# Reading and writing a matmul's columns alternately from two halves, in runs of two

## The chip, the cores and the metric

One core of a Trainium2 chip runs the whole program. The metric is device time in microseconds (us), the median of several runs. The kernel before has 2062.7 us, from three runs of 2062.58, 2063.46 and 2062.70 us.

## The reference, cut to what matters

One inference step of a two-layer decoder trunk, for 512 prompt tokens and 8 x 4 sample tokens (544 tokens, model width 1024, hidden width 2816). Everything is float32.

```
h = h + 0.5 * swiglu(rmsnorm(h, ffn1_norm[i]), w1, w3, w2)      # four such FFNs, two a layer
xn = rmsnorm(h, mix_norm[i])
layer 0: mix = (u * (w_s @ rmsnorm(v) + b_s)) @ w_out,  u, v = split(xn @ w_in)    # gMLP
layer 1: mix = attention(rmsnorm(xn @ w_q), shared k, v, log-forget) @ w_o         # forgetting attention
h = h + mix
h = h + 0.5 * swiglu(rmsnorm(h, ffn2_norm[i]), w1, w3, w2)
h = h + sigmoid(rmsnorm(h, ple_norm[i]) @ w_gate) * (pe[i] @ w_proj)               # gated embedding (PLE)
after layer 0: k, v, logf = shared_kv(h)
...
swiglu(x, w1, w3, w2) = (silu(x @ w1) * (x @ w3)) @ w2
```

## The kernel before, in words

The activations lie transposed: 128 features on the partitions, 544 tokens along the free dimension. A float32 product is made of three products in the type fp32r (float32 operands, read by TensorE in reduced precision): both operands are split into a high and a low part, and high x high, high x low and low x high are summed in one PSUM accumulator. The text calls each of the three a *split product*: one MATMUL with 128 x 128 weights (loaded by its own LDWEIGHTS) and a moving operand of 128 partitions by N tokens. 15,724 of the 16,442 MATMULs in the trace are such fp32r products; the others are transposes, the small float32 products of the gMLP's spatial gate, of the statistics and of the sample tokens' attention.

Three groups of lines hold nearly all of them. `mm` (lines 241, 245 and 247) is the plain product over all 544 tokens: since a PSUM bank has room for 512 columns, the tokens are cut by `COLS` at `CUT` into 256 and 288 columns, and `whole` places the two pieces on both sides of the border between the two banks of a `ps` tile. `products` inside `ffn_steps` (line 491) holds the FFN's first two weights in a seven-product form (a Strassen-like scheme on token halves and on halves of the inner dimension): it works on halves of `HT` = 272 tokens already. The remaining split products are the statistics (`rstd`, line 362), the last tile (`cols_mm`, 675), the value projection (`v_group`, 829 to 831, 256 columns), the scores and outputs of the attention (`qk`, 1107 to 1115, and `pv`, 1159 to 1161, 256 to 512 columns) and the output projection (`product`, 1268 to 1275, 272 columns).

VectorE (DVE) and ScalarE (ACT) split weights and activations, evacuate PSUM and do the elementwise work beside TensorE; weights come by DMA from the SyncE (SP) queue. In the FFNs the order of work is written out by hand (a slot list, run under a manual schedule); elsewhere the framework's scheduler sets it. Operands are read, and results written, in ascending address order in all these products:

```
i = nc.tensor.matmul(out[:, a:b], wh, xh[:, a:b], start=s, stop=False)
```

Of the kernel before, what the change touches and what calls it, by code (L numbers as in the profile page):

```python
# [82 lines left out]

CUT = 256
COLS = ((0, CUT), (CUT, T))


def whole(p):  # L90
# [4 lines left out]
class Builder:  # L95
# [133 lines left out]
    def mm(self, out, w, x, first, last, mid=None):  # L229

        nc = self.nc
        out = whole(out)
        n = len(w)
        pin, self.pins = self.pins > 0 and first, self.pins - first
        for k in range(n):
            (wh, wl), (xh, xl) = w[k], x[k]
            if mid is not None and k == n - 1:
                mid()
            s, e = first and k == 0, last and k == n - 1
            for a, b in COLS:  # L240
                i = nc.tensor.matmul(out[:, a:b], wh, xh[:, a:b], start=s, stop=False)  # L241
                if pin and k == 0:
                    self.tc.keep_in_program_order(i)
            for a, b in COLS:
                nc.tensor.matmul(out[:, a:b], wh, xl[:, a:b], start=False, stop=False)  # L245
            for a, b in COLS:
                nc.tensor.matmul(out[:, a:b], wl, xh[:, a:b], start=False, stop=e)  # L247

    def tile_mm(self, xs, mid=None):

# [103 lines left out]
    def rstd(self, acc):  # L354

        parts = self.tmp(F32R), self.tmp(F32R)
        self.nc.scalar.copy(parts[0], acc)
        self.nc.vector.tensor_tensor(parts[1], acc, parts[0].bitcast(F32), ALU.subtract)
        sums = [self.pb()[:, :HT] for _ in range(2)]
        for n, x in enumerate(parts):  # L360
            for a, ps in enumerate(sums):
                self.nc.tensor.matmul(ps, self.onesr, x[:, a * HT:(a + 1) * HT], start=n == 0, stop=n == 1)
        r = self.st()
        assert self.chain is None
        self.chain = self.rsqrt_steps(r, sums, D)
        next(self.chain)
        return r
# [97 lines left out]
    def ffn_steps(self, h, xf, rstd, hid, todo, plain, on_chunk):  # L465
# [8 lines left out]
        def products(j, k, part):  # L474
            if k == "1" and j not in tiles:
                tiles[j] = {}
            t = tiles[j]
            if k in "152" and "ABC"["125".index(k)] not in t:
                if k == "2":
                    t["B"] = [self.pb()[:, :HT] for _ in range(2)]  # L480
                else:
                    t["A" if k == "1" else "C"] = self.ps()[:, :, :HT]
            out = t["A" if k in "1674" else "C" if k in "53" else "B"]
            dst = out if k == "2" else [out[:, w] for w in range(2)]
            hi, lo = self.take()
            for kp in range(NKP):
                xh, xl = xf[kp][k]
                for n, (a, b) in enumerate(((hi, xh), (hi, xl), (lo, xh))):
                    for w in range(2):
                        c = slice(512 * w + P * kp, 512 * w + P * kp + P)  # L490
                        nc.tensor.matmul(dst[w], a[:, c], b, start=k in "152" and kp == 0 and n == 0,  # L491
                                         stop=kp == NKP - 1 and n == 2, skip_group_check=True)
            after.append(lambda: evict(j, k))

# [175 lines left out]
    def cols_mm(self, outs, w, x):  # L670

        for (a, b), out in zip(COLS, outs):
            for k, ((wh, wl), (xh, xl)) in enumerate(zip(w, x)):
                for n, (u, v) in enumerate(((wh, xh), (wh, xl), (wl, xh))):
                    i = self.nc.tensor.matmul(out[:, :b - a], u, v[:, a:b], start=k == 0 and n == 0,
                                              stop=k == len(w) - 1 and n == 2)
                    if k == n == a == 0:
                        self.tc.keep_in_program_order(i)
# [89 lines left out]
    def kv(self, h, box, ffn_gain):  # L768
# [40 lines left out]
        def v_group(g, beside):  # L809
# [13 lines left out]
            for i in range(4):  # L823
                if i % 2 == 0:
                    self.advance()
                t, out = slice(i * P, i * P + P), p[:, 256 * i:256 * i + 256]
                for k, (wh, wl) in enumerate(w):
                    xh, xl = xs[k]
                    nc.tensor.matmul(out, xh[:, t], wh, start=k == 0, stop=False)  # L829
                    nc.tensor.matmul(out, xh[:, t], wl, start=False, stop=False)  # L830
                    nc.tensor.matmul(out, xl[:, t], wh, start=False, stop=k == NC_ - 1)  # L831
                for f in beside[i]:
                    f()
            for i in range(4):
# [245 lines left out]
    def attention(self, xs, acc, h_out, on_chunk):  # L1080
# [19 lines left out]
        def qk(h):  # L1100
            kp, _ = st["kv", h]
            qp = st.pop(("q", h))
            S = [self.ps(), self.ps()]
            for i in range(4):
                out = S[i // 2][:, i % 2, :]
                w, qs = W[i], slice(i * P, (i + 1) * P)
                nc.tensor.matmul(out[:, :w], self.L[h % 4][:, qs], self.R[:, 0, :w],
                                 start=True, stop=False)
                nc.tensor.matmul(out[:, :w], qp[:, 0, qs], kp[:, 0, :w], start=False, stop=False)
                nc.tensor.matmul(out[:, :w], qp[:, 0, qs], kp[:, 1, :w], start=False, stop=False)  # L1110
                nc.tensor.matmul(out[:, :w], qp[:, 1, qs], kp[:, 0, :w], start=False, stop=False)
                if i == 0:
                    nc.tensor.matmul(out[:, :256], self.identr, self.neg[:, 128:384], start=False, stop=True)
                else:
                    nc.tensor.matmul(out[:, (i - 1) * P:(i + 1) * P], self.identr, self.neg[:, 0:256],
                                     start=False, stop=True)
            if h < 4:
                self.fetch_term(h + 4)
            ps = []
            for i in range(4):  # L1120
                w = (i + 1) * P
                sc = S[i // 2][:, i % 2, :w]
                m, l = self.sm(1), self.sm(1)
                p = self.tmp()
                nc.vector.tensor_reduce(m, sc, AX.X, ALU.max, negate=True)
                nc.scalar.activation(p[:, :w], sc, AF.Exp, bias=m, accum_out=l)
                nc.vector.reciprocal(l, l)
                if i in (1, 2):
                    nc.gpsimd.tensor_scalar(p[:, :w], p[:, :w], l, None, ALU.mult)
                else:  # L1130
                    nc.scalar.activation(p[:, :w], p[:, :w], AF.Copy, scale=l)
                ps.append(p)
            st["p", h] = ps
# [17 lines left out]
        def pv(h):  # L1151
# [4 lines left out]
            for j, (t3, c0, n) in enumerate(mv):  # L1156
                vs = slice(j * P, (j + 1) * P)
                out = acc[:, 512 - n:512]
                nc.tensor.matmul(out, vp[:, 0, vs], t3[:, 0, c0:c0 + n], start=j == 0, stop=False)
                nc.tensor.matmul(out, vp[:, 0, vs], t3[:, 1, c0:c0 + n], start=False, stop=False)  # L1160
                nc.tensor.matmul(out, vp[:, 1, vs], t3[:, 0, c0:c0 + n], start=False, stop=j == 3)
            o[h] = self.big(F32R)
            self.split_pair(o[h], acc, slice(0, SEQ))

# [94 lines left out]
            for a in range(2):  # L1259
                nc.sync.dma_start(out=st["vs"][NS * a:NS * a + NS], in_=self.vsd[:, 512 * a:512 * a + 512])  # L1260

        def product(out, hs, w, ks, late=False):
            hi, lo = w
            pin, self.pins = self.pins > 0, 0
            for n, k in enumerate(ks):
                c = slice(P * n, P * n + P)
                s, e = n == 0, n == len(ks) - 1
                i = nc.tensor.matmul(out, hi[:, c], o[k][:, 0, hs], start=s, stop=False)  # L1268
                if pin and s:
                    self.tc.keep_in_program_order(i)  # L1270
                if not late:
                    nc.tensor.matmul(out, hi[:, c], o[k][:, 1, hs], start=False, stop=False)  # L1272
                nc.tensor.matmul(out, lo[:, c], o[k][:, 0, hs], start=False, stop=e and not late)  # L1273
            for n, k in enumerate(ks if late else ()):
                nc.tensor.matmul(out, hi[:, P * n:P * n + P], o[k][:, 1, hs], start=False, stop=n == len(ks) - 1)

        def project_half(c, part):

# [1 line left out]
            hi, lo = self.unit()  # L1280
            for a in range(2):
                w = slice(4 * P * a, 4 * P * a + 4 * P)
                product(p[:, a, :HT], slice(0, HT), (hi[:, w], lo[:, w]), range(4 * part, 4 * part + 4))
            out = self.hp[c][:, :, :HT]
            behind = st.pop(("sel", 1), None)
            with self.tc.issue_after(behind.ins) if behind else nullcontext():
# [4 lines left out]
        def project(c):  # L1291

            p = self.ps()
            self.pins = c == 0
            product(p[:, 0, :HT], slice(HT, T), self.unit(), range(NH), late=c == 0)
            out = h_out[c][:, HT:]
            nc.vector.tensor_tensor(out, p[:, 0, :HT], out, ALU.add)
            on_chunk(c, slice(HT, T))
# [230 lines left out]
```

## Time and profile before

| what | value |
|---|---|
| median of three runs | 2062.7 us |
| the profiled execution's span, first to last instruction | 2060.8 us |
| around the span, by the median | 1.9 us |
| TensorE (PE), busy share of the span | 99% |
| weight loads (PEld), busy share | 98% |
| VectorE (DVE), busy share | 73% |
| ScalarE (ACT), busy share | 46% |
| GpSimd (POOL), busy share | 9% |
| mean DMA rate | 115 GB/s |

The profiled execution's own device time is not given apart from its span, so its time is taken as the span and the 1.9 us around it.

How to read it: PE's busy time is no measure of its rate. MATMULs overlap, and the profile models their ends: a product has a "duration" of 288 ns while the next one starts 125 ns after it. What a product costs is the distance from its start to the next one's start, read from rows that give a time and a count (the chain in order of time, or the timeline of TensorE).

### The profile page before, as it was taken

The page shows a single profiled execution, that of the slowest core. Times are in us where ns is not written, and L with a number is a line of the kernel's source. Part 1 is how long each engine was busy: PE and PEld are TensorE (multiplying, and loading weights), DVE is VectorE, ACT ScalarE, POOL GpSimd, SP SyncE. Part 2 cuts the span into 40 slices and gives each one's busy share as a digit, 9 for nine tenths or more (in the row PEclk, how much of TensorE's full clock was granted, in tenths as well). Part 3 has the DMA queues.
Part 4 walks back from the last instruction along what each step waited for, and adds up shares of the span by engine and source line. Part 5 has one row for each costly group of instructions (what it writes and reads, how often), then busy time and mean ns, then how long its engine had stood idle before and what let it go on. Part 6 is the DMA issues. An engine that isn't in the chain of part 4 may idle for free.

```text
span 2060.8 us, 38864 instructions
## 1 busy us (share of the span) xinstructions
PE 2045.6 (99%) x16442; PEld 2013.9 (98%) x16442; DVE 1506.0 (73%) x1862; ACT 950.9 (46%) x1421; POOL 185.6 (9%) x222
## 2 busy tenths in 40 slices
PE   9999999999999999999999999999999999999999
PEld 8999999999999999999999999999987999999999
DVE  7877777556687778776688777776476888777774
ACT  7535344423554344454456343534364754344451
POOL 0000000410100000043060000001131200000020
PEclk9999999999999999999999999999999999999999
DMA  5233234312223232432374323324669232222421
GB/s 185 84 111 107 74 109 141 97 45 83 83 93 113 72 104 82 154 99 82 103 261 161 113 86 110 107 66 136 192 211 320 96 100 84 102 103 82 130 97 44
DMA packets 93823, 237.95 MB, mean 115 GB/s; under 512 B 9538, under 2 KB 27490, under 8 KB 93650
## 3 DMA queue, kind: packets, MB, share of 16 engines
q1 hardware_dynamic: 93506, 235.44, 34.3%
q8 instruction: 129, 2.11, 0.4%
q14 instruction: 44, 0.36, 0.0%
q10 hardware_dynamic: 144, 0.04, 0.0%
HBM read 218.95 MB, written 16.49 MB: 114 GB/s over the span
## 4 chain that ended last, share of the span: by engine, by line
PE 92%; DVE 3%; ACT 2%; issue 1%; DMA 1%; SPq 0%; POOL 0%; DVEq 0%; ACTq 0%; POOLq 0%
PE ps L491 33%; PE ps L241 16%; PE ps L247 16%; PE ps L245 15%; PE pb L491 5%; DVE big L199 1%; ACT big L198 1%; PE ps L1268 1%; PE ps L1273 1%; PE ps L1272 1%; DVE big L184 0%; PE ps L1223 0%; PE ps L829 0%; PE ps L830 0%; PE ps L831 0%
## 5 line engine op out<-in xcount | busy, mean ns | idle before, releaser
L491 PE MATMUL ps<-big,big 128*128 128x272 f32 x5616 | 727.6, 288 | 1.8 <-DVE big L508 1.3
L491 PEld LDWEIGHTS ps<-big,big 128*128 128x128 f32 x5616 | 714.2, 188 | 2.4 <-issue 1.6
L199 DVE TENSOR_TENSOR big<-big,big 128x1024 fp32r<-128x1024 f32 (+2 forms) x538 | 590.8, 1100 | 106.4 <-ACT big L198 106.0
L198 ACT CAST big<-big 128x1024 fp32r<-128x1024 f32 (+2 forms) x538 | 488.0, 932 | 267.8 <-DVE big L184 262.5
L241 PE MATMUL ps<-big,big 128*128 128x256 f32 (+1 forms) x2684 | 558.2, 289 | 1.2 <-ACT big L198 0.8
L247 PE MATMUL ps<-big,big 128*128 128x256 f32 x2684 | 554.0, 288 | 1.9 <-DVE big L199 1.9
L245 PE MATMUL ps<-big,big 128*128 128x256 f32 x2684 | 553.8, 287 | 0.1
L241 PEld LDWEIGHTS ps<-big,big 128*128 128x128 f32 x2684 | 429.8, 188 | 5.3 <-issue 1.7
L247 PEld LDWEIGHTS ps<-big,big 128*128 128x128 f32 x2684 | 429.3, 188 | 3.7 <-DVE big L199 3.2
L245 PEld LDWEIGHTS ps<-big,big 128*128 128x128 f32 x2684 | 432.3, 189 | 0.5 <-DVE big L298 0.5
L326 POOL TENSOR_TENSOR st<-st,tmp 128x544 f32<-128x544 f32 (+1 forms) x63 | 89.0, 1412 | 1587.0 <-ACT tmp L324 1586.8
L530 DVE SCALAR_TENSOR_TENSOR big<-ps,big 128x544 f32<-128x544 f32 x160 | 115.5, 722 | 106.6 <-PE ps L247 106.4
L184 DVE TENSOR_TENSOR big<-big,big 128x1024 f32<-128x1024 f32 x156 | 190.0, 1218 | 0.0
L499 ACT COPY tmp<-ps 128x544 f32<-128x544 f32 x117 | 71.9, 614 | 141.3 <-PE ps L491 141.3
L454 ACT ACTIVATE big<-big 128x544 f32<-128x544 f32 x88 | 58.0, 660 | 163.0 <-DVE big L451 161.8
L491 PE MATMUL pb<-big,big 128*128 128x272 f32 x936 | 124.0, 288 | 0.0
L451 DVE TENSOR_TENSOR big<-big,st 128x1088 f32<-128x1088 f32 x88 | 113.3, 1289 | 10.6 <-ACT big L513 8.9
L491 PEld LDWEIGHTS pb<-big,big 128*128 128x128 f32 x936 | 120.2, 188 | 0.0
L286 DVE TENSOR_TENSOR big<-big,big 128x544 fp32r<-128x544 f32 (+1 forms) x112 | 81.5, 734 | 36.7 <-ACT big L285 36.5
L297 ACT ACTIVATE big<-big,gains 128x544 fp32r<-128x544 f32 (+1 forms) x80 | 55.6, 704 | 105.9 <-DVE big L530 64.9
L298 DVE SCALAR_TENSOR_TENSOR big<-big,gains,big 128x544 fp32r<-128x544 f32 (+1 forms) x80 | 66.7, 843 | 25.2 <-ACT big L297 25.2
L285 ACT CAST big<-big 128x544 fp32r<-128x544 f32 (+1 forms) x112 | 71.3, 644 | 16.2 <-DVE big L457 8.9
(213 smaller groups left out, 1436.5 us busy)
## 6 DMA issues: line engine op xcount, KB each, us to landing
big<-in_w SPq DMA_DIRECT2D x156, 512.0 KB
big<-in_w2a SPq DMA_DIRECT2D x64, 512.0 KB
big<-in_w2b SPq DMA_DIRECT2D x32, 384.0 KB
big<-in_w13p SPq DMA_DIRECT2D x16, 512.0 KB
big<-in_win SPq DMA_DIRECT2D x16, 512.0 KB
big<-in_wg SPq DMA_DIRECT2D x16, 512.0 KB
big<-in_ck SPq DMA_DIRECT2D x16, 512.0 KB
big<-in_cv SPq DMA_DIRECT2D x16, 512.0 KB
```

The source lines that it names most:

```text
L184: self.nc.vector.tensor_tensor(t, a, b, ALU.add if op == "+" else ALU.subtract)
L198: self.nc.scalar.copy(hi, src)
L199: self.nc.vector.tensor_tensor(lo, src, hi.bitcast(F32), ALU.subtract)
L241: i = nc.tensor.matmul(out[:, a:b], wh, xh[:, a:b], start=s, stop=False)
L245: nc.tensor.matmul(out[:, a:b], wh, xl[:, a:b], start=False, stop=False)
L247: nc.tensor.matmul(out[:, a:b], wl, xh[:, a:b], start=False, stop=e)
L286: self.nc.vector.tensor_tensor(pair[:, 1, cols], src, pair[:, 0, cols].bitcast(F32), ALU.subtract)
L326: nc.gpsimd.tensor_tensor(acc[:, cols], acc[:, cols], sq, ALU.add)
L451: tt(g, g, rstd.unsqueeze(1).broadcast_to([P, 2, T]), ALU.mult)
L491: nc.tensor.matmul(dst[w], a[:, c], b, start=k in "152" and kp == 0 and n == 0, stop=kp == NKP - 1 and n == 2, skip_group_check=True)
L499: nc.scalar.copy(t["r" + k], t["C" if k == "5" else "A"])
L530: nc.vector.scalar_tensor_tensor(h[c], whole(out), 0.5, h[c], ALU.mult, ALU.add)
```

## The change

Two functions are added. `woven` views an access pattern of N columns as pairs from two halves: columns 0 and 1, then N/2 and N/2 + 1, then 2 and 3, then N/2 + 2 and N/2 + 3, and so on. `product` issues the MATMUL with this view on the moving operand and on the result, so that each sum still arrives in its own place. All 15,724 split products go through `product`; transposes and float32 products do not. With it `CUT` goes from 256 to `HT` = 272, so the token pieces in `mm` and in the last tile are 272 and 272 and not 256 and 288. An inner function named `product` is renamed `products`.

```diff
-CUT = 256
+CUT = HT
 COLS = ((0, CUT), (CUT, T))
+def woven(ap):
+    return ap.rearrange("p (a b c) -> p b a c", a=2, c=2)
+def product(nc, out, w, x, **k):
+    return nc.tensor.matmul(woven(out), w, woven(x), **k)
...
             for a, b in COLS:
-                i = nc.tensor.matmul(out[:, a:b], wh, xh[:, a:b], start=s, stop=False)
+                i = product(nc, out[:, a:b], wh, xh[:, a:b], start=s, stop=False)
...
-                        nc.tensor.matmul(dst[w], a[:, c], b, start=k in "152" and kp == 0 and n == 0,
+                        product(nc, dst[w], a[:, c], b, start=k in "152" and kp == 0 and n == 0,
                                          stop=kp == NKP - 1 and n == 2, skip_group_check=True)
...
-                    nc.tensor.matmul(out, xh[:, t], wh, start=k == 0, stop=False)
+                    product(nc, out, xh[:, t], wh, start=k == 0, stop=False)
...
-                nc.tensor.matmul(out[:, :w], qp[:, 0, qs], kp[:, 0, :w], start=False, stop=False)
+                product(nc, out[:, :w], qp[:, 0, qs], kp[:, 0, :w], start=False, stop=False)
```

The same replacement is made on all the other lines named above.

No instruction is added or taken away, and the order stays on every engine; what changes on TensorE is the pattern. Line numbers below line 86 move up by 10 or 11, and all split products carry line 97, that of `product`. In the first FFN tile of `mm` TensorE had these rows, one weight block (`ps_190` the accumulator, `big_120` the moving operand, `big_123` and `big_124` the high and low weights):

```order
L241 MATMUL ps_190<-big_120,big_123 128x256
L241 MATMUL ps_190<-big_120,big_123 128x288
L245 MATMUL ps_190<-big_120,big_123 128x256
L245 MATMUL ps_190<-big_120,big_123 128x288
L247 MATMUL ps_190<-big_120,big_124 128x256
L247 MATMUL ps_190<-big_120,big_124 128x288
```

Now it has the following ones for this and the next two blocks (68 steps, two halves, two columns):

```order
L97 MATMUL ps_190<-big_120,big_123 128x68x2x2 x4
L97 MATMUL ps_190<-big_120,big_124 128x68x2x2 x2
L97 MATMUL ps_190<-big_127,big_123 128x68x2x2 x4
L97 MATMUL ps_190<-big_127,big_124 128x68x2x2 x2
L97 MATMUL ps_190<-big_130,big_123 128x68x2x2 x4
L97 MATMUL ps_190<-big_130,big_124 128x68x2x2 x2
```

The six products of a block are the same as before and in the same order; the widths 256 and 288 became 272, and the pattern has two more dimensions.

At the program's end the last output tile is finished in two pieces (`tmp_23525` the gate, `pb_...` and `ps_...` the accumulators, `big_95` the residual stream). VectorE had there:

```order
L688 TENSOR_TENSOR tmp_23525<-pb_23526,st_23050 128x256
L688 TENSOR_TENSOR tmp_23525<-pb_23527,st_23050 128x288
L693 TENSOR_TENSOR tmp_23525<-ps_23580,tmp_23525 128x256
L694 TENSOR_TENSOR big_95<-big_95,tmp_23525 128x256
L693 TENSOR_TENSOR tmp_23525<-ps_23581,tmp_23525 128x288
L694 TENSOR_TENSOR big_95<-big_95,tmp_23525 128x288
```

and now has:

```order
L698 TENSOR_TENSOR tmp_23525<-pb_23526,st_23050 128x272
L698 TENSOR_TENSOR tmp_23525<-pb_23527,st_23050 128x272
L703 TENSOR_TENSOR tmp_23525<-ps_23580,tmp_23525 128x272
L704 TENSOR_TENSOR big_95<-big_95,tmp_23525 128x272
L703 TENSOR_TENSOR tmp_23525<-ps_23581,tmp_23525 128x272
L704 TENSOR_TENSOR big_95<-big_95,tmp_23525 128x272
```

The two pieces are equal now; nothing else moved there.

More of the change, by code (lines that the diff above doesn't have):

```diff
@@ L244, in mm @@
             for a, b in COLS:
-                nc.tensor.matmul(out[:, a:b], wh, xl[:, a:b], start=False, stop=False)
+                product(nc, out[:, a:b], wh, xl[:, a:b], start=False, stop=False)
             for a, b in COLS:
-                nc.tensor.matmul(out[:, a:b], wl, xh[:, a:b], start=False, stop=e)
+                product(nc, out[:, a:b], wl, xh[:, a:b], start=False, stop=e)
     def tile_mm(self, xs, mid=None):
@@ L361, in rstd @@
             for a, ps in enumerate(sums):
-                self.nc.tensor.matmul(ps, self.onesr, x[:, a * HT:(a + 1) * HT], start=n == 0, stop=n == 1)
+                product(self.nc, ps, self.onesr, x[:, a * HT:(a + 1) * HT], start=n == 0, stop=n == 1)
         r = self.st()
@@ L674, in cols_mm @@
                 for n, (u, v) in enumerate(((wh, xh), (wh, xl), (wl, xh))):
-                    i = self.nc.tensor.matmul(out[:, :b - a], u, v[:, a:b], start=k == 0 and n == 0,
+                    i = product(self.nc, out[:, :b - a], u, v[:, a:b], start=k == 0 and n == 0,
                                               stop=k == len(w) - 1 and n == 2)
@@ L828, in v_group @@
                     xh, xl = xs[k]
-                    nc.tensor.matmul(out, xh[:, t], wh, start=k == 0, stop=False)
-                    nc.tensor.matmul(out, xh[:, t], wl, start=False, stop=False)
-                    nc.tensor.matmul(out, xl[:, t], wh, start=False, stop=k == NC_ - 1)
+                    product(nc, out, xh[:, t], wh, start=k == 0, stop=False)
+                    product(nc, out, xh[:, t], wl, start=False, stop=False)
+                    product(nc, out, xl[:, t], wh, start=False, stop=k == NC_ - 1)
                 for f in beside[i]:
@@ L1106, in qk @@
                 w, qs = W[i], slice(i * P, (i + 1) * P)
-                nc.tensor.matmul(out[:, :w], self.L[h % 4][:, qs], self.R[:, 0, :w],
+                product(nc, out[:, :w], self.L[h % 4][:, qs], self.R[:, 0, :w],
                                  start=True, stop=False)
-                nc.tensor.matmul(out[:, :w], qp[:, 0, qs], kp[:, 0, :w], start=False, stop=False)
-                nc.tensor.matmul(out[:, :w], qp[:, 0, qs], kp[:, 1, :w], start=False, stop=False)
-                nc.tensor.matmul(out[:, :w], qp[:, 1, qs], kp[:, 0, :w], start=False, stop=False)
+                product(nc, out[:, :w], qp[:, 0, qs], kp[:, 0, :w], start=False, stop=False)
+                product(nc, out[:, :w], qp[:, 0, qs], kp[:, 1, :w], start=False, stop=False)
+                product(nc, out[:, :w], qp[:, 1, qs], kp[:, 0, :w], start=False, stop=False)
                 if i == 0:
-                    nc.tensor.matmul(out[:, :256], self.identr, self.neg[:, 128:384], start=False, stop=True)
+                    product(nc, out[:, :256], self.identr, self.neg[:, 128:384], start=False, stop=True)
                 else:
-                    nc.tensor.matmul(out[:, (i - 1) * P:(i + 1) * P], self.identr, self.neg[:, 0:256],
+                    product(nc, out[:, (i - 1) * P:(i + 1) * P], self.identr, self.neg[:, 0:256],
                                      start=False, stop=True)
@@ L1158, in pv @@
                 out = acc[:, 512 - n:512]
-                nc.tensor.matmul(out, vp[:, 0, vs], t3[:, 0, c0:c0 + n], start=j == 0, stop=False)
-                nc.tensor.matmul(out, vp[:, 0, vs], t3[:, 1, c0:c0 + n], start=False, stop=False)
-                nc.tensor.matmul(out, vp[:, 1, vs], t3[:, 0, c0:c0 + n], start=False, stop=j == 3)
+                product(nc, out, vp[:, 0, vs], t3[:, 0, c0:c0 + n], start=j == 0, stop=False)
+                product(nc, out, vp[:, 0, vs], t3[:, 1, c0:c0 + n], start=False, stop=False)
+                product(nc, out, vp[:, 1, vs], t3[:, 0, c0:c0 + n], start=False, stop=j == 3)
             o[h] = self.big(F32R)
@@ L1260, in load_vs, with products @@
                 nc.sync.dma_start(out=st["vs"][NS * a:NS * a + NS], in_=self.vsd[:, 512 * a:512 * a + 512])
-        def product(out, hs, w, ks, late=False):
+        def products(out, hs, w, ks, late=False):
             hi, lo = w
@@ L1267, in product @@
                 s, e = n == 0, n == len(ks) - 1
-                i = nc.tensor.matmul(out, hi[:, c], o[k][:, 0, hs], start=s, stop=False)
+                i = product(nc, out, hi[:, c], o[k][:, 0, hs], start=s, stop=False)
                 if pin and s:
@@ L1271, in product @@
                 if not late:
-                    nc.tensor.matmul(out, hi[:, c], o[k][:, 1, hs], start=False, stop=False)
-                nc.tensor.matmul(out, lo[:, c], o[k][:, 0, hs], start=False, stop=e and not late)
+                    product(nc, out, hi[:, c], o[k][:, 1, hs], start=False, stop=False)
+                product(nc, out, lo[:, c], o[k][:, 0, hs], start=False, stop=e and not late)
             for n, k in enumerate(ks if late else ()):
-                nc.tensor.matmul(out, hi[:, P * n:P * n + P], o[k][:, 1, hs], start=False, stop=n == len(ks) - 1)
+                product(nc, out, hi[:, P * n:P * n + P], o[k][:, 1, hs], start=False, stop=n == len(ks) - 1)
         def project_half(c, part):
@@ L1282, in project_half @@
                 w = slice(4 * P * a, 4 * P * a + 4 * P)
-                product(p[:, a, :HT], slice(0, HT), (hi[:, w], lo[:, w]), range(4 * part, 4 * part + 4))
+                products(p[:, a, :HT], slice(0, HT), (hi[:, w], lo[:, w]), range(4 * part, 4 * part + 4))
             out = self.hp[c][:, :, :HT]
@@ L1294, in project @@
             self.pins = c == 0
-            product(p[:, 0, :HT], slice(HT, T), self.unit(), range(NH), late=c == 0)
+            products(p[:, 0, :HT], slice(HT, T), self.unit(), range(NH), late=c == 0)
             out = h_out[c][:, HT:]
```

## The prediction

> **What bounds the kernel now.** I read the page first (busy shares, clock, the chain of work that ended last), then the chain in order of time, then the timeline of TensorE at the few places where products of other widths stand side by side, last the waits and the stages.
>
> ```profile
> span 2060.8 us, 38864 instructions
> PE 2045.6 (99%) x16442; PEld 2013.9 (98%) x16442; DVE 1506.0 (73%) x1862; ACT 950.9 (46%) x1421; POOL 185.6 (9%) x222
> ...
> PEclk9999999999999999999999999999999999999999
> ...
> PE 92%; DVE 3%; ACT 2%; issue 1%; DMA 1%; SPq 0%; POOL 0%; DVEq 0%; ACTq 0%; POOLq 0%
> ```
>
> TensorE is on 92% of the chain, at a granted clock that never falls below nine tenths in a slice. Its waits are small; these two are the longest in total:
>
> ```profile
> PE ps L247 <- DVE big L199: 1.9, 4, 0.5
> PE ps L1107 <- ACT tmp L1126: 1.6, 4, 0.5
> ```
>
> So the time is the number of products times the distance from one start to the next. The chain in order of time (start, length, what) gives that distance in the long unbroken runs, one in each of the four FFNs:
>
> ```profile
> 311.15 15.03 PE ps L491 x120
> ...
> 838.92 15.03 PE ps L491 x120
> ...
> 1378.10 15.03 PE ps L491 x120
> ...
> 1927.65 15.03 PE ps L491 x120
> ```
>
> 15.03 us for 120 products of 272 columns is 125.3 ns each, the same to 0.1 ns in four FFNs in which other engines and the DMAs do other things at that moment. What sets it lies in the product itself, not in contention. Is it the least possible? The timeline of TensorE in the attention has products of 256 and of 512 columns, and in the gMLP four float32 transposes of 128 columns:
>
> ```profile
> 1511.30 0.28 PE L1107 MATMUL ps<-big,big 128*128 128x256 f32 x1
> 1511.42 0.28 PE L1109 MATMUL ps<-big,big 128*128 128x256 f32 x1
> 1511.54 0.28 PE L1110 MATMUL ps<-big,big 128*128 128x256 f32 x1
> 1511.65 0.28 PE L1111 MATMUL ps<-big,big 128*128 128x256 f32 x1
> 1511.77 0.27 PE L1115 MATMUL ps<-neg,identr 128*128 128x256 f32 x1
> ...
> 1514.44 0.40 PE L1107 MATMUL ps<-big,big 128*128 128x512 f32 x1
> 1514.67 0.39 PE L1109 MATMUL ps<-big,big 128*128 128x512 f32 x1
> 1514.90 0.40 PE L1110 MATMUL ps<-big,big 128*128 128x512 f32 x1
> 1515.14 0.39 PE L1111 MATMUL ps<-big,big 128*128 128x512 f32 x1
> 1515.37 0.27 PE L1115 MATMUL ps<-neg,identr 128*128 128x256 f32 x1
> ```
> ```profile
> 446.61 0.60 PE L618 MATMUL ps<-consts,big 128*128 128x128 f32 x4
> 447.05 0.27 PE L619 MATMUL ps<-consts,big 128*32 128x128 f32 x1
> ```
>
> 256 columns take 0.47/4 = 117.5 ns, 512 take 0.93/4 = 232.5 ns: 0.449 ns a column and 2.5 ns a product. A transpose takes 0.44/4 = 110 ns; less the same 2.5 ns that is 0.84 ns a column, twice the pace of a full-rate column if that were 0.42 ns. So a split product of 272 columns would take 272 x 0.42 + 2.5 = 116.7 ns at exactly twice the transposes' pace, and takes 125.3 ns. Some 8.6 ns of each product (7%) are lost in streaming its columns, in proportion to their number. That surplus is what a new order of columns can touch; nothing else in the profile is worth as much.
>
> **The change, part by part.** Its reach: these groups (count behind the x) are the bulk.
>
> ```profile
> L491 PE MATMUL ps<-big,big 128*128 128x272 f32 x5616 | 727.6, 288 | 1.8 <-DVE big L508 1.3 <-ACT tmp L499 0.5
> L491 PE MATMUL pb<-big,big 128*128 128x272 f32 x936 | 124.0, 288 | 0.0
> L241 PE MATMUL ps<-big,big 128*128 128x256 f32 (+1 forms) x2684 | 558.2, 289 | 1.2 <-ACT big L198 0.8
> ```
>
> 5616 + 936 in the seven-product form, 3 x 2684 = 8052 in `mm` (lines 245 and 247 have as many), and 1,120 in the small groups: 15,724 products. One nanosecond on each is 15.7 us.
>
> *The woven pattern.* No row of before reads or writes with a hop, so its price is unknown and is bounded. Below: all of the surplus goes, 116.7 ns, -8.6 x 15.7 = -135 us. Above, by the nearest row at all: the transposes' pace, 272 x 0.84 + 2.5 = 231 ns, +106 x 15.7 = +1,660 us. Which end is nearer? The loss is regular, the same in every FFN, and grows with the columns; so it looks like a stall that comes back every so many neighbouring columns of an ascending stream. Two streams half a product apart, taken in turn, change just that: each walks at half the pace, and the next pair never lies behind the last one. With halves of 272 tokens the streams lie 136 columns apart everywhere in the FFNs and in `mm`. I take about two thirds of the surplus as won, 5.8 ns, so 119.5 ns a product: -91 us. I take it below the full 8.6 since a fixed part and the weight loads may hold some back: weight loads are seen to keep up with a product every 117.5 ns (the 256-column rows above, each with its own load), and not faster with this operand.
>
> *Halves of 272 for 256 and 288 in `mm`.* The sum of columns stays at 544. The timeline's steady stretch of `mm`:
>
> ```profile
> 439.14 0.41 PE L241 MATMUL ps<-big,big 128*128 128x256 f32 x2
> ...
> 446.37 0.41 PE L247 MATMUL ps<-big,big 128*128 128x256 f32 x2
> ```
>
> lies 7.23 us, or 29 pairs, apart: 249.3 ns a pair, against 250.6 for two of line 491's. At line 491's pace 4,026 pairs would lose 1.3 ns each, 5 us; at equal price per column, nothing. I take 0, inside the other term's bounds. The evacuations by VectorE and ScalarE read all 544 columns as before: 0. At the very end the second piece is 16 columns shorter for each of VectorE, ScalarE and the DMA, some hundredths of a us: 0.
>
> *What is late next.* The partners have slack, but less with a faster TensorE. One FFN stage:
>
> ```profile
> core 0: us, PE busy (x) PEld busy (x) DVE busy (x) ACT busy (x) POOL busy (x), PEclk, DMA share, GB/s
> ...
> 1090.00:1450.00 360.00, 359.51 (x2871) 359.07 (x2870) 276.09 (x315) 163.77 (x224) 13.23 (x13) 1.00 0.32 104
> ```
>
> VectorE works 276 of 360 us (77%). At 119.5 ns a product the stage takes some 343 us and VectorE is at 80%; at the floor of 116.7 ns, 335 us and 82%. It would not be the bound on the mean, but its splits (line 199) are waited for a little oftener. I add 4 us over the whole kernel. Weights come at 104 GB/s there, with the DMA engines a third busy: hidden.
>
> Sum, against the profiled execution's own time (span 2060.8 and 1.9 us around it, which is the median of the runs, 2062.7): 2062.7 - 91 + 4 = 1976, say **1975 us**.
>
> **Rivals.**
>
> *The hop costs and brings nothing.* If the surplus comes per column and not from the order of addresses, the pattern is neutral and only the new cut is left: 2062.7 to 2068 us (0 to +5 above). For it: the surplus is equal in reading different tiles, and I have no row that shows its cause. The Trainium skill says in "SBUF — State Buffer" (Specifications, cachelines) that a read keeps its full rate with at least two hits on each line of 16 bytes; runs of two float32 columns just do, so by that rule the sum is this rival's 2063 to 2068. No run here shows it yet.
>
> *Every line is entered twice, and that is what costs.* If the surplus is the price of moving on to a new short stretch of addresses, then a stretch longer than two columns is now left and entered again. Entered twice for once, the 8.6 ns become 17.2: +135 us, 2198 us; more often, more. The place is every split product; the point from which it decides is any price above zero for the return to a stretch that has been left, since TensorE has no slack on 92% of the chain. Against it: a stream in turn from two places gives each place twice the time. The same page of the Trainium skill speaks for this rival in the second half of its rule, that each cross to a new line pays. This is my case of the other sign.
>
> *The write side breaks.* The result is written with the same hops. If PSUM took a broken-up row at the transposes' pace, a product would take 231 ns and the kernel 2062.7 + 1,660 = 3,720 us. For it speaks only that no row of before writes PSUM in this way; no row points to it either, and so it gets the smallest chance. The Trainium skill, "PSUM — Partial Sum Buffer", Specifications, says that any non-contiguous access pattern slows matmuls significantly, in 8-byte lines; by that rule the sum would be some such figure, and no run here shows it yet.
>
> *The whole surplus goes:* 2062.7 - 135 + 8 for later partners = 1936 us; the lower end of my own case.
>
> **How the numbers follow.** A stall is removed, wholly or in part: 0.58, between 1920 and 2050, with 1975 the likeliest. Neutral: 0.14, 2058 to 2070. Doubled moves: 0.21, spread from 2070 to 2300 around 2198. Half pace: 0.07. About 0.2% (4 us) is what a measurement of this kernel can tell from no change: faster 0.59 (the first case and a sliver of the second), same 0.11, slower 0.30 (the last two and a sliver of the second). The range 1915 to 2200 leaves out the half pace, the upper half of the doubled moves (some 0.1) and next to nothing below. The likeliest case's own range is 1920 to 2050.
>
> **What would show it.** In the profile after, the long runs of the FFNs in the chain, now on line 97, are to have 120 products in about 14.3 us (14.0 at the floor, 15.0 if neutral, 16.1 if moves are doubled, 27.7 at half pace), with all four FFNs alike again. The first-to-last distance in `mm` has to shrink by the same share; transposes stay at 110 ns. VectorE's and ScalarE's busy times stay at 1506 and 951 us, with larger shares. TensorE's waits for line 199's splits may grow from 1.9 us to several. I am wrong if products at other widths (256 in the value projection, 512 in the attention) and 272 in the FFNs move in different directions, which would mean that the distance between the halves decides and not the pairs; or if the products stay at 125 ns, or grow.

## The result, and the profile after

The changed kernel takes 2844.5 us (median of four runs, 2844.4 to 2844.7) against 2063.1 us before: ratio 1.379, 95% interval 1.377 to 1.381. It is 38% slower, +781 us. The forecast of 1975 us was wrong in sign, and the time lies outside the range of 1915 to 2200 us.

The page of the changed kernel: span, engines, clock, and the chain that ended last.

```profile
span 2842.9 us, 38871 instructions
...
PE 2835.4 (100%) x16442; PEld 2797.3 (98%) x16442; DVE 1510.0 (53%) x1862; ACT 943.0 (33%) x1421; POOL 180.9 (6%) x222
...
PEclk9999999999999999999999999999999999999999
...
PE 99%; DVE 0%; ACT 0%; DMA 0%; issue 0%; SPq 0%; DVEq 0%
```

As many MATMULs (16,442), the same granted clock, the same work for VectorE and ScalarE (1510 and 943 us, before 1506 and 951). TensorE hardly waits for the others any more: its share of the chain went from 92 to 99%. The longest unbroken run in the chain in order of time (start, length, what) now has 492 products, and TensorE's timeline in the attention has the 512-column products:

```profile
1271.17 86.36 PE ps L97 x492
```
```profile
2086.58 1.48 PE L97 MATMUL ps<-big,big 128*128 128x512 f32 x4
2087.89 0.33 PE L97 MATMUL ps<-neg,identr 128*128 128x256 f32 x1
```

86.36/492 is 175.5 ns for a product of 272 columns, 125.3 ns before. Four of 512 columns are (2087.89 - 2086.58)/4 = 327.5 ns apart, before 232.5. Both widths lose 0.18 to 0.19 ns a column. 50.2 ns on each of 15,724 products are 789 us; TensorE's idle time in the span (span less busy time) fell from 15.2 to 7.5 us, which takes off 8, and that is the loss of 781 us. So the whole loss lies in the pace of the products; what is open is why the pattern costs this.

### The profile page after: what moved, and what is told of

The parts are those of the page before. It is cut to its first block, busy times and chain, and to the rows that moved or that the text cites. A ratio compares the mean times of both kernels' runs of the same rounds, so it can differ in the third digit from the quotient of the medians.

```text
span 2842.9 us, 38871 instructions
## 1 busy us (share of the span) xinstructions
PE 2835.4 (100%) x16442; PEld 2797.3 (98%) x16442; DVE 1510.0 (53%) x1862; ACT 943.0 (33%) x1421; POOL 180.9 (6%) x222
## 4 chain that ended last, share of the span: by engine, by line
PE 99%; DVE 0%; ACT 0%; DMA 0%; issue 0%; SPq 0%; DVEq 0%
PE ps L97 90%; PE pb L97 7%; PE ps L1233 0%; PE ps L639 0%; PE pb L1194 0%; PE pb L757 0%; PE ps L1151 0%; PE pb L850 0%; DMA big<-in_w13p 0%; PE ps L628 0%; PE pb L1151 0%; PE ps L642 0%; ACT tmp L1136 0%; PE ps L1240 0%; ACT big L208 0%; PE pb L891 0%
## 5 line engine op out<-in xcount | busy, mean ns | idle before, releaser
L97 PE MATMUL ps<-big,big 128*128 128x272 f32 (+1 forms) x14576 | 2586.0, 353 | 2.1 <-ACT tmp L1136 0.9
L97 PEld LDWEIGHTS ps<-big,big 128*128 128x128 f32 x14576 | 2554.2, 196 | 16.9 <-issue 4.9
L97 PE MATMUL pb<-big,big 128*128 128x272 f32 (+3 forms) x1080 | 205.0, 357 | 0.1
L97 PEld LDWEIGHTS pb<-big,big 128*128 128x128 f32 x1080 | 190.5, 196 | 4.1 <-ACT big L295 0.3
L523 ACT COPY big<-ps 128x544 f32<-128x544 f32 x39 | 23.9, 612 | 224.5 <-PE ps L97 224.5
L518 DVE TENSOR_TENSOR big<-ps,tmp 128x544 f32<-128x544 f32 x39 | 28.3, 725 | 98.8 <-PE ps L97 98.8
L520 DVE TENSOR_TENSOR big<-ps,tmp 128x544 f32<-128x544 f32 x39 | 28.3, 725 | 75.4 <-PE ps L97 75.4
L467 DVE TENSOR_TENSOR big<-big 128x544 f32<-128x544 f32 x88 | 62.9, 718 | 1.6 <-ACT big L464 1.6
L516 DVE TENSOR_TENSOR big<-pb,tmp 128x272 f32<-128x272 f32 x78 | 30.8, 436 | 53.0 <-PE pb L97 53.0
L334 ACT ACTIVATE tmp<-big 128x544 f32<-128x544 f32 (+1 forms) x63 | 37.3, 594 | 52.4 <-DVE big L607 36.4
```

The costliest lines, as they stand in the source:

```text
L97: return nc.tensor.matmul(woven(out), w, woven(x), **k)
L467: tt(g[:, 1], g[:, 1], g[:, 0], ALU.mult)
```

## The experiments

All but the last start from the changed kernel and change `woven` and the view on the result, here called `landed`; the last one starts from the kernel before. Times of before, run beside them, were 2061.8 to 2062.8 us.

### Which side pays, and what the cut costs

```diff
 def product(nc, out, w, x, **k):
-    return nc.tensor.matmul(woven(out), w, woven(x), **k)
+    return nc.tensor.matmul(landed(out), w, woven(x), **k)
...
+    return ap.rearrange("p (b a c) -> p b a c", a=2, c=2)     # ascending order
```

A side that is to go in ascending order gets the last line as its view, written with as many dimensions as the woven one: `landed` in the read-only run, `woven` in the write-only run, both in the run with the cut only. The other side keeps the pairs in turn.

Read only:

> Only the moving operand is read in the woven order; the result is written in ascending order (so the sums of the split products land in permuted columns). Before, a product of 272 columns came every 125.6 ns; with both sides woven, every 175.6 ns: 50 ns for 136 pairs. Theory R (the read pays: each pair makes the read enter its stretch of addresses again): all of the 50 ns stay, about 2845 us. Rival W (the write to PSUM pays): 125 to 126 ns a product, 2060 to 2070 us. Rival A (each inner loop of an access pattern costs its address generator something, on either side): some part on each side, between 2200 and 2845 us, with the read-only and write-only surpluses adding up.

Write only:

> Only the result is written in the woven order; the operand is read in ascending order (sums land in permuted columns). Theory R (the read pays): 125 to 126 ns a product, 2060 to 2070 us. Rival W (the write pays): 175 ns a product, about 2845 us. Rival A (both address generators pay, side by side): as the slower of the two if they run at the same time, so up to 2845 us too.

The cut only:

> Token halves of 272 for 256 and 288, and no woven pattern: ascending columns on both sides. All theories: 0 to +5 us by the two paces of before (249.3 ns a pair of pieces in the plain product, 250.6 ns for two products of the seven-product form), so 2063 to 2068 us. If more than 5 us of the 781 us come from the cut, part of the loss has nothing to do with the pattern.

Measured: 2844.7 us (ratio 1.379, 1.377 to 1.381), 2069.2 us (1.0032, 1.0020 to 1.0044) and 2069.7 us (1.0036, 1.0022 to 1.0049). The longest run of products in the chain of each, read only, write only, cut only:

```profile
1271.32 86.36 PE ps L102 x492
```
```profile
919.60 61.75 PE ps L102 x492
```
```profile
919.37 61.75 PE ps L102 x492
```

The read alone has the changed kernel's 86.36 us to the last digit; the write with its hops has the ascending order's 61.75 us (125.5 ns a product). So the read pays everything and the write nothing. Rival W is out, and so is a second payment in the write's address generator. The Trainium skill says in "PSUM — Partial Sum Buffer", Specifications, that any non-contiguous pattern slows matmuls significantly; the write-only run differs by 0.5 us from the one that writes in ascending order, so for pairs of neighbouring columns, at this pace of 125.5 ns, this run does not bear that out. The cut by itself costs 6.9 us (2069.7 against 2062.8): two pieces of 272 are slower than 256 and 288.

### Longer runs

```diff
-    return ap.rearrange("p (a b c) -> p b a c", a=2, c=2)
+    return ap.rearrange("p (a b c) -> p b a c", a=2, c=4)     # and c=8
```

Runs of four columns:

> Both sides woven in runs of four columns (16 bytes) in place of two; same halves. Theory R in the form that a read takes stretches of 16 bytes and pays for a second entry: no stretch is entered twice, so the surplus is gone: 125 to 127 ns a product, 2060 to 2085 us. A price per hop, whatever the length of the run (rival A, and W as a price per hop): half as many hops, 25 ns of the 50 left, 150 ns a product, about 2455 us. A price for alternating between two far places at all: stays near 2845 us.

Runs of eight:

> Halves in turn, in runs of eight columns (32 bytes) on both sides: 34 hops a product. Runs of four left 5.0 ns a product over the ascending order (2147.7 against 2069.7 us), 0.07 ns a hop. If that rest is a price of each hop: 2.5 ns left, 2105 to 2115 us. If it is a price of taking turns between two streams at all: still 5 ns, about 2148 us. If it comes from a 16-byte line being entered without its neighbour of 32 bytes: gone, 2065 to 2075 us.

Measured: 2147.7 us (ratio 1.041, 1.040 to 1.043) and 2131.3 us (1.033, 1.032 to 1.035). Chain of runs of four, and of eight:

```profile
954.53 64.33 PE ps L102 x492
```
```profile
948.47 63.42 PE ps L102 x492
```

130.8 and 128.9 ns a product. With four columns, 16 bytes, in a row, 45 of the 50 ns are gone, though there are still 68 hops for 136: it isn't the hop that costs. A rest of 5 ns stays and falls only to 3.4 ns when the hops halve again; a price per hop (2.5 ns expected), a fixed one (5 ns) and a missing neighbour of 32 bytes (nothing left) all fail to fit it, and its cause stays open.

### One stream with steps, and two near places

```diff
-    return ap.rearrange("p (a b c) -> p b a c", a=2, c=2)
+    return ap.rearrange("p (b a c) -> p a b c", a=2, c=2)     # steps, both sides
+    # near: as the change, with the second place 4 columns behind the first for 136, read side
```

Steps:

> Pairs again, but no alternation between halves: a product takes pairs 0, 2, 4, ... (columns 0 1, 4 5, 8 9, ...) in one ascending pass and pairs 1, 3, 5, ... in a second one, on both sides. Theory L (the read is paid for by the 16-byte line: each entry into a line takes at least (175.6 - 2.5)/136 = 1.27 ns, whatever was read before; four columns of a line in a row at 0.45 ns hide it, two do not): 136 entries a product as in the change, 173 to 177 ns, 2820 to 2860 us. Rival B (the two places that are read in turn disturb each other, as by lying in the same bank): no second place, 125 to 128 ns, 2065 to 2110 us.

Near:

> Read side only, ascending write: pairs are taken in turn from two places 4 columns (16 bytes) apart, not 136, so columns 0 1, 4 5, 2 3, 6 7, 4 5, 8 9, ...; columns 0 to 139 are read twice and the others not at all. Theory L with one line held: three of four pairs change the line (the fourth has four columns of it in a row): 2 x 1.27 + 1.8 = 4.3 ns for eight columns, 150 ns a product, about 2450 us. Theory L with two lines or more held: no change costs anything, 125 to 127 ns, 2065 to 2090 us. Rival B: two near places in different lines of the same neighbourhood, no reason to be better than halves, 175 ns, 2845 us, unless the distance decides.

Measured: 3900.2 us (ratio 1.891, 1.888 to 1.894) and 1966.9 us (0.954, 0.952 to 0.955). The chain of the steps, and of the near places:

```profile
1748.88 119.19 PE ps L102 x492
```
```profile
1330.52 57.27 PE ps L105 x484
```

Steps take 242.3 ns a product; I had expected 175. Theory L in its first form (1.27 ns an entry, whatever came before) is wrong: without any second place a line of 16 bytes of which only two columns are used costs more, (242.3 - 2.5)/136 = 1.76 ns, 2.5 being the fixed part of a product from the prediction. Rival B is wrong too: with no second place it expected 125 to 128 ns. And with two places in neighbouring lines the read is *faster* than in ascending order, 118.3 ns against 125.5. The reading of this that the next runs test: there a line, once read, serves both places, so a line is fetched in about 1.76 ns and kept for a while. Four columns at full rate last 1.67 ns ((115.8 - 2.5)/272 a column, by the next run). That would also be a reason why the ascending order stays behind full rate: it needs a line every 1.67 ns and gets one every 1.76. It covers the larger part, about 6 ns of the 9.7 (125.5 less 115.8).

### Runs of one column

```diff
+    return ap.rearrange("p (a b) -> p b a", a=2)              # halves; a=4 quarters, a=8 eighths
+    return ap.rearrange("p (b a) -> p a b", a=2)              # columns 0, 2, 4 ..., then 1, 3, 5 ...
```

All with an ascending write, so that the sums land in permuted columns. Halves:

> Read side only, halves in turn in runs of one column: 272 entries into a line for each product, one column from each. Theory L (1.27 ns an entry): 272 x 1.27 + 2.5 = 348 ns a product, +222 ns x 15,724 = +3,490 us, about 5,560 us. If a column that is alone costs less than an entry of a pair (the price counts bytes, not entries): not over 2845 us. If it costs more (a half-used 8-byte word pays on top): over 5,700 us.

Quarters:

> Read side only, runs of one column, from four quarters in turn (columns 0, 68, 136, 204, 1, 69, ...). Runs of one from two halves took 116 ns a product, faster than ascending order (125 ns) and than runs of two (175 ns). Theory E (columns of even and of odd place in the stream are read by two separate lanes, and a lane is slow when it changes its line at each access: from halves in runs of one each lane goes through one half in ascending order, in runs of two each lane hops between the halves): with four quarters each lane hops again, about 175 ns, 2845 us or more. Rival S (single columns are read in another way than adjacent pairs, and hops cost them nothing): 116 ns, about 1936 us.

Even columns, then odd ones:

> Read side only, runs of one column and no second place: columns 0, 2, 4, ... 270 and then 1, 3, 5, ... 271. Theory E: one lane takes 0, 4, 8, ..., the other 2, 6, 10, ..., both in the same line of 16 bytes and in a new one at each access, as with pairs in steps of four columns (242 ns a product): about 240 ns, 3900 us. Rival S: 116 ns, about 1936 us. A price per line of a single ascending stream, whatever the lanes (one line for two columns): also 240 ns; then the run with quarters tells E from it.

Pairs again, 64 bytes apart:

> Read side only: pairs in turn from two places 16 columns (64 bytes) apart; columns 0 to 151 are read, most of them twice, but the second time 8 pairs later and not 2 as in the run with 4 columns (118 ns a product, 1966.9 us). If that run was fast because the two places were near: 118 to 120 ns, 1965 to 2000 us. If it was fast because the line of one place is the next line of the other, so that a line just read serves twice: 175 ns as with halves, about 2845 us.

Measured, in one run each: 1935.8, 2371.1, 3899.7 and 2842.6 us. Their chains, in this order:

```profile
1307.90 56.06 PE ps L102 x484
```
```profile
1056.47 71.34 PE ps L102 x492
```
```profile
1748.41 119.19 PE ps L102 x492
```
```profile
1270.49 86.10 PE ps L105 x492
```

Runs of one from two halves gave the surprise: 115.8 ns, all the surplus gone, where 348 ns had been expected. Theory L, that counts each entry into a line, was dead with it. Rival S (single columns go another way and hops cost them nothing) fell with even and odd columns: 242.3 ns, as with the pairs in steps. 64 bytes apart, pairs cost 175 ns as with halves: so it was not a distance of at most 64 bytes that made the near places fast; the second use of a line just read fits. Quarters took 145.0 ns, between the 116 of rival S and the 175 of theory E, so theory E missed here as well. That middle value shaped the last form of the theory, **E2**: the read has two lanes, one for the even and one for the odd places of the stream; each lane keeps two lines of 16 bytes, and fetches the lines it needs next one at a time, in about 1.75 ns each, into the place of the line whose last use lies further back.

### How many lines a lane keeps, and the order put to use

Eighths:

> Read side only, runs of one column from eight eighths in turn. Theory E2: each lane goes round four lines with room for two, so every access loads a line anew: 236 to 242 ns a product, as slow as the steps, about 3850 to 3900 us. Rival C (more lines are held, and what costs is that first entries into lines come bunched: four quarters cost 29 ns more than two halves, 145 against 116 ns): the bunches double and come half as often: 145 to 150 ns, 2370 to 2450 us.

Pairs 32 bytes apart:

> Read side only, pairs in turn from two places 8 columns (32 bytes) apart. Between 4 columns (118 ns a product, a line of the second place is the first place's next one, used at once) and 16 columns (175 ns). Theory E2: with two lines held the second place's line is gone when the first place reaches it: 172 to 178 ns, 2790 to 2890 us. Rival C (four lines or more held a lane): still there, 116 to 120 ns, 1940 to 2000 us.

Measured, in one run each: 3793.4 and 2840.6 us; their chains:

```profile
1695.55 115.89 PE ps L102 x492
```
```profile
1270.30 86.23 PE ps L105 x492
```

235.5 and 175.3 ns a product, where theory E2 gave 236 to 242 and 172 to 178, and rival C 145 to 150 and 116 to 120. Both speak for E2, the first just below its range. Take the change as an example of how E2 is worked out. Of every eight columns a lane takes four, each lasting two columns' time, 0.83 ns; it needs two new lines for them, 3.5 ns one after the other. Both places being taken, it can start the first fetch only after its last column from the old line of the first half. When the second new line has come, two more columns go by (one from this line, then the last from the other) before the next fetch can start. So eight columns take 3.5 + 2 x 0.83 = 5.17 ns in place of 3.33, and a product 34 x 5.17 + 2.5 = 178 ns. In the same way, with two lanes, two lines and 1.75 ns, for all orders tried (ns a product):

| order of the read | E2 | measured |
|---|---|---|
| ascending | 121.5 | 125.5 |
| halves, runs of two (the change) | 178 | 175.5 |
| halves, runs of four, of eight | 121.5 | 130.8, 128.9 |
| halves, runs of one | 116 | 115.8 |
| quarters, runs of one | 147 | 145.0 |
| eighths, runs of one | 240 | 235.5 |
| pairs in steps; even, then odd | 240 | 242.3; 242.3 |
| two places 16 bytes apart | 120 | 118.3 |
| two places 32, 64 bytes apart | 178 | 175.3, 175.0 |

A single lane with two lines would give some 207 ns for halves in runs of one, so the lanes are needed for that row. The price of a line was taken from the pairs in steps and the form of E2 from the rows up to the quarters; only the eighths, the places 32 bytes apart and the version that follows were forecast by it. It is a theory that fits, and nothing here shows lanes or lines directly. It misses the ascending order by 4 ns and the longer runs by 7 to 9. One rival was not tried: the places 32 and 64 bytes and half a product apart are all an even number of 16-byte lines apart, and the fast ones 16 bytes apart are one line, an odd number. Pairs from places three lines apart would tell whether even or odd plays a part.

Last, the fast order in a version that computes the reference. No run writes in runs of one. Here the result is written in ascending order, which leaves the columns of the two halves in turn in PSUM, and the readers put them back.

```diff
+def woven(ap):
+    return ap.rearrange("p (a b) -> p b a", a=2)
+def nat(ap):
+    return ap.rearrange("p (a b) -> p a b", a=2)
+def whole4(p):
+    return whole(p).rearrange("p (b a) -> p a b", a=2)
...
+    return nc.tensor.matmul(landed(out[:, q * HT:q * HT + HT]), w, woven(x)[:, b], **k)    # b: 136 of 272 pairs
...
-                nc.vector.scalar_tensor_tensor(h[c], whole(out), 0.5, h[c], ALU.mult, ALU.add)
+                nc.vector.scalar_tensor_tensor(nat(h[c]), whole4(out), 0.5, nat(h[c]), ALU.mult, ALU.add)
```

> A version that computes the reference: in the plain product, the seven-product form and the output projection (14,988 products) the operand is read from two halves in runs of one column, the result is written in ascending order, and VectorE and ScalarE put the columns back when they read PSUM (every second column, then the others). Theory E2 (two lanes, one for even and one for odd columns of the stream, each with two lines of 16 bytes held and one load of a line at a time in 1.7 to 1.8 ns): 116 ns a product, as in the look with runs of one (1935.8 us for all 15,724), so 1943 us if the readers of PSUM pay nothing for their steps. If they pay and it comes onto the chain: up to 2000 us. Rival: the pace of 116 ns came from sums that are not used in their order, or from the other small groups: no gain, 2063 to 2070 us.

Measured: 1938.1 us (1937.7 to 1938.4, five runs), ratio 0.9398, 0.9385 to 0.9410. It beats the kernel before by 124 us. Its page, a long run in the plain product and, by form, a reader of PSUM on VectorE and one on ScalarE, first in this version and then in the kernel before:

```profile
span 1935.2 us, 38865 instructions
...
PE 1912.5 (99%) x16442; PEld 1878.0 (97%) x16442; DVE 1501.2 (78%) x1862; ACT 947.1 (49%) x1421; POOL 186.9 (10%) x222
...
PE 86%; DVE 7%; ACT 4%; issue 2%; DMA 1%; SPq 0%; POOL 0%; DVEq 0%; ACTq 0%
```
```profile
362.94 43.32 PE ps L138 x374
```
```profile
L581 DVE SCALAR_TENSOR_TENSOR big<-ps,big 128x544 f32<-128x544 f32 x160 | 115.3, 721 | 75.9 <-PE ps L138 75.9
...
L550 ACT COPY tmp<-ps 128x544 f32<-128x544 f32 x117 | 71.5, 612 | 89.7 <-PE ps L102 89.7
```
```profile
L530 DVE SCALAR_TENSOR_TENSOR big<-ps,big 128x544 f32<-128x544 f32 x160 | 115.5, 722 | 106.6 <-PE ps L247 106.4
...
L499 ACT COPY tmp<-ps 128x544 f32<-128x544 f32 x117 | 71.9, 614 | 141.3 <-PE ps L491 141.3
```

43.32/374 is 115.8 ns a product, here with the two places 272 columns apart and not 136. Before, the two readers took 722 and 614 ns, now 721 and 612: reading every second column of PSUM costs them nothing. TensorE's share of the chain is 86%, VectorE's 7: the partners begin to come onto the path. TensorE's idle time in the span is 22.7 us (1935.2 less 1912.5), 7.5 us more than before.

## Why the prediction was wrong, point by point

*The bound* was read rightly. The time is the number of products times their distance, and the time lost in streaming the columns could be had back: the version with runs of one is at 1938 us, where the prediction's "whole surplus" case stood at 1936. That these two lie so close is in part chance: the pace went to 115.8 ns, below the floor of 116.7, on only 14,988 of the 15,724 products. The weight loads, for which 2.8 ns were held back, kept up with 115.8 ns.

*The step that failed* is the choice between the two ends of the woven pattern's price. The bounds, 116.7 and 231 ns, held the measured 175.5. I took 119.5, near the lower one, from an argument without a row: that a stall which comes back with the columns would go if two streams took turns. The runs show in its place that the read pays for taking turns in pairs: 50.0 ns a product more than in ascending order (175.5 against 125.5, all of it on the read side). Of these 45 are gone with runs of four columns, 16 bytes, and in runs of one, with twice as many hops, a product takes 115.8 ns, less than in ascending order. Theory E2 gives a mechanism that fits: what repeats is the fetch of a line of 16 bytes, in about 1.75 ns, hidden by the columns taken from that line before it is left. By it taking turns does help, but in runs of one; in runs of two each lane goes back and forth between two lines, needs both, and has no room to fetch the next.

*The rival "every line is entered twice"* named the right side and the right kind of cost, and the wrong size: it gave 8.6 ns more a product, 2198 us, and 50 were measured. It took the visible surplus for the whole price of a line, when by E2 it is only the part of the price that sticks out from behind four columns. That was the mis-sized term, and the upper end of the range hung on it. The Trainium skill's rule in "SBUF — State Buffer" (Specifications, cachelines) on which the neutral rival was hung, full rate from two hits a line on, fails here if a hit is taken for a column; its line of 16 bytes fits the step from runs of two to runs of four (175.5 to 130.8 ns).

*The cut of 272* was put at 0 with a bound of 5 us; it is 6.9 us (the cut-only run). The pace of line 491, which I had beside it, was the better price.

*What is late next:* the 4 us for VectorE never came up, since TensorE slowed; where it did speed up, in the version with runs of one, VectorE's work stayed at 1501 us and TensorE's idle time grew by 7.5 us, close to the 8 that the "whole surplus" case allowed for later partners.

*The write side* was rightly held for unlikely: in pairs it costs nothing that the time shows (2069.2 against 2069.7 us).

*The chances* gave 0.58 to a stall removed, though no row of before had shown a hop; the case that had the right side, moves that cost, got 0.21.

## What to carry to other kernels

When a fully streaming matmul runs a few per cent behind its own best pace, look at the order in which it reads its columns: for these fp32r operands, reading one column in turn from each of two halves brought 6% here, and the same idea in runs of two cost 38%. A price that is hidden shows only its overhang; before doubling the number of such events, work out the whole price, or measure one event that nothing hides. And where no row of the trace shows an access pattern, hold both bounds open instead of choosing the end that the argument likes.

## What the runs showed of the hardware

The order of the moving operand's columns alone moves an fp32r product of 272 columns between 115.8 and 242.3 ns. Where each pair of columns comes from a new line of 16 bytes (pairs in steps), a pair costs 1.76 ns, against 0.83 for two columns at the best pace seen. Pairs in turn from two places cost the same at 32 bytes, 64 bytes and half a product (175.3, 175.0 and 175.5 ns); at 16 bytes they are faster than the ascending order (118.3 ns). Hops in pairs when writing PSUM, and steps of two columns when VectorE and ScalarE read it, cost nothing measurable (2069.2 against 2069.7 us; 721 against 722 and 612 against 614 ns).
